# Latent attention: where the products of branch a stand among the steps of the heads

## The chip, the cores and the metric

The kernel runs on one core of one Trainium2 chip. The metric is the device time of one execution in microseconds (us). The kernel before was timed three times: 971.97, 972.13 and 969.66 us, median 971.97 us. The profiled execution, a fourth one, took 969.88 us, of which its instructions span 968.1 us.

## The reference

One decoder layer on 1024 tokens of width 1024, float32. The part that matters:

```python
o_a = stick_breaking_attention(...)             # branch a, 8 heads
y_a = (o_a * silu(sb_z)) @ w_branch_a           # 512 -> 1024
q, k, v = ...                                   # from the two latents, 8 heads, 64 + 32 wide
sc = (q_nope @ k_nope + q_pe @ k_pe) * scale    # causal
o_b = softmax(sc) @ v                           # branch b, latent attention
y_b = (o_b * silu(mla_z)) @ w_branch_b          # 512 -> 1024
merged = sigmoid(g_a) * y_a + sigmoid(g_b) * y_b
x = x + gate * (merged @ w_out); return rmsnorm(x, final_norm_gain)
```

## The kernel before, in words

Every product of float32 values is made of three products of rounded parts (high x high, high x low, low x high), each 128 rows by up to 512 columns on TensorE (PE). The kernel goes through its stages in this order: the opening, branch a's attention with other projections beside it, the two latents, the up-projections, the eight heads of the latent attention, then one closing stage that makes y_b, merges it with y_a, multiplies by w_out and normalizes.

**The products of branch a.** y_a is made by eight jobs, one for each block of 128 output columns, each of two units of 512 tokens: 16 units in all. A unit is 12 products (4 blocks of 128 inputs, three parts), L301, `ps_g<-oa,whi` and `ps_g<-oa,wlo`. VectorE (DVE) then multiplies the unit's result by the gate read back from DRAM (`gl<-ps_g,gl`, L1019) and the sync engine's DMA queue (SP) stores it (`ya_d<-gl`, L1020). Before a job its weights are loaded (L274), DVE rounds them (L88) and GpSimd (POOL) takes the rest (L96). Two buffers hold gates, two hold loaded weights, two PSUM tiles (`ps_g`) hold results. The units come out of a generator, one at each call of `advance(filler, 1)`; two are called in the up-projection (UQF, L1126), the others among the heads.

**The heads.** `mla_heads` (L1207) is a generator too. Each head `h` has eight rows `i` of 128 queries. A row of scores (L1166) is, for each piece of up to 512 keys, three products (L1179 to L1181) into one of two `ps_s` tiles, from which DVE takes the scaled, masked score and the running maximum (L1182); ScalarE (ACT) takes the exponential (L1191). Four rows later PE turns the row in blocks of 128 (L702, `ps_t<-ident,sc`), ACT and DVE write its two parts out (L86, L96), and after each second row PE multiplies by the values (L719, `ps_o<-wth,vb`). Each head begins with eight turns of its queries (L1156). The sums of the exponentials are turned (L1200), go to DRAM and come back spread over the rows (`rs_d`, `rb`, L1203 and L1204); in the last head this is done by halves, POOL multiplies by the gate (L1237) and DVE scales the output (L1238).

The generator stops 128 times, at each row of scores and at each row that is turned. The loop at the end counts these steps. FP is a list of steps at which one more unit is called; from step IA on a unit is called inside `issue_after(anchor)`, which puts each of the unit's instructions on PE behind the last product of the heads issued so far. Below IA, and on all other engines, a scheduler that runs when the program is built may move the unit to an earlier place. What is left of the units after the heads is called at once (L1294).

**The closing stage.** y_b has eight jobs of two units each as well (L301, `<-ob,whi`), whose tiles lie in memory that the heads gave back. For each unit SP loads a gate (`gbl`, L1309) and the stored y_a (`yal`, L1310), DVE multiplies and adds (L1311, L1312), ACT and DVE split the sum. Between these loads SP also issues the loads of w_branch_b (`raw`, L274) and of w_out (`rawo`, L1326), all in one order fixed when the program is built.

Of the kernel before, what the change touches and what calls it, by code (L numbers as in the profile page):

```python
# [48 lines left out]
def hybrid_layer(ctx: ExitStack, tc: tile.TileContext, x, c, positions, w_ada, b_ada, norm_gain, w_in,  # L49
# [853 lines left out]
    with tc.tile_pool(name="latw", bufs=2, **RW, side="right") as lp:  # L903
# [32 lines left out]
        for t in range(NT):  # L936
# [13 lines left out]
            v = small.tile([P, 2], F32, name="vl", tag="vl")  # L950
# [325 lines left out]
            pump()  # L1276

    step, done, total = 0, 0, 2 * len(yajobs) - len(UQF) - UQE
    FP = [int(v) for v in "1 1 5 7 33 36 43 91 103 123 124 132 132".split()]
    IA = 110  # L1280
    heads = mla_heads()
    while True:
        if not advance(heads, 1):
            break
        step += 1
        want = sum(step >= v for v in FP) if FP else min(total, total * step // YSTEPS)
        if want > done:
            if step >= IA:
                with tc.issue_after(anchor[0].ins):
# [137 lines left out]
```

## Time and profile before

| | |
|---|---|
| runs of the kernel before | 971.97, 972.13, 969.66 us |
| profiled execution: time, span | 969.88 us, 968.1 us |
| PE busy, weight loads (PEld) busy | 98%, 85% of the span |
| DVE, ACT, POOL busy | 65%, 45%, 30% |
| chain that ended last | PE 93%, DMA 4%, DVE 1% |
| heads of the latent attention | from about 667 to 831 us |
| closing stage | from about 831 us to the end |

Times in the rows are us from the start of the span. PE's products overlap: a row of 0.39 us may be followed by the next after 0.23 us, so PE looks busy even where it could go faster; the spacing of starts says more than the busy time. A row "[0.88 <-ACT whi L86]" means that the engine sat idle that long before it and what ended the wait. PEclk is the granted clock of PE, 1.00 for 2.4 GHz and 0.50 for 1.2 GHz. DMA is the mean busy share of the 16 DMA engines.

### The profile page before, as it was taken

What the parts mean: (1) busy time and instruction counts of PE and PEld (TensorE: products, weight loads), DVE (VectorE), ACT (ScalarE), POOL (GpSimd) and SP (SyncE); (2) the same over time, 40 slices, a digit from 0 to 9 for tenths busy, and PEclk for the clock granted to TensorE, in tenths of its full rate; (3) what the DMA queues carried; (4) which work ended last, traced back from release to release, by engine and by line L of the source; (5) the groups of instructions that cost most, each with busy time, mean ns of one, the idle gap of its engine ahead of it and who ended that gap; (6) DMA issues with size and microseconds to landing.
All of it is one profiled execution on the core that took longest, in us unless ns stands there. A gap on an engine that the chain in (4) does not pass through costs nothing.

```text
span 968.1 us, 14331 instructions
## 1 busy us (share of the span) xinstructions
PE 945.7 (98%) x5132; PEld 818.4 (85%) x5132; DVE 633.2 (65%) x1277; ACT 440.2 (45%) x991; POOL 287.8 (30%) x271
## 2 busy tenths in 40 slices
PE   4999999999999999999999999999999999989997
PEld 4888888888888888888888999988899998868886
DVE  5757747586747873584564544964699997696654
ACT  5454433353435343444352423643588885342211
POOL 1010145444634554445352001611121441001222
PEclk9999999999999999999999999999999999999999
DMA  9911643215321322113123301689553422792233
GB/s 307 338 74 44 221 149 99 77 44 163 98 66 44 115 71 77 25 53 98 56 86 111 99 2 33 226 280 291 162 155 102 115 86 88 262 357 96 71 120 99
DMA packets 112711, 122.38 MB, mean 126 GB/s; under 512 B 14928, under 2 KB 81597, under 8 KB 112256
## 3 DMA queue, kind: packets, MB, share of 16 engines
q1 hardware_dynamic: 112550, 121.44, 40.1%
q8 instruction: 41, 0.67, 0.3%
q14 instruction: 30, 0.25, 0.1%
q10 hardware_dynamic: 90, 0.02, 0.0%
HBM read 86.80 MB, written 34.64 MB: 125 GB/s over the span
## 4 chain that ended last, share of the span: by engine, by line
PE 93%; DMA 4%; DVE 1%; ACT 0%; issue 0%; SPq 0%; POOL 0%; DVEq 0%; ACTq 0%; POOLq 0%
PE ps_g L301 37%; PE ps_o L719 7%; PE ps_t L702 7%; PE ps_g L944 3%; PE ps_g L1363 3%; PE ps_s L1363 3%; PE ps_t L1363 3%; PE ps_s L945 3%; PE ps_g L553 3%; PE ps_s L553 2%; PE ps_s L1179 2%; PE ps_s L1181 2%; PE ps_s L1180 2%; PE ps_s L750 2%; PE ps_s L749 2%; PE ps_t L1059 2%
## 5 line engine op out<-in xcount | busy, mean ns | idle before, releaser
L301 PE MATMUL ps_g<-hh,whi 128*128 128x512 f32 x448 | 177.7, 397 | 0.0
L301 PE MATMUL ps_g<-hl,whi 128*128 128x512 f32 x448 | 176.9, 395 | 0.0
L301 PE MATMUL ps_g<-hh,wlo 128*128 128x512 f32 x448 | 175.7, 392 | 0.0
L753 DVE TENSOR_TENSOR_SCAN surv<-surv,diag 128x128 f32<-128x128 f32 (+3 forms) x64 | 109.6, 1717 | 47.6 <-ACT surv L751 46.5
L96 POOL TENSOR_TENSOR wlo<-raw,whi 128x1024 fp32r<-128x1024 f32 (+1 forms) x36 | 78.0, 2166 | 113.9 <-DVE whi L88 36.3
L96 DVE TENSOR_TENSOR wtl<-ps_t,wth 128x512 fp32r<-128x512 f32 (+1 forms) x192 | 101.7, 548 | 11.0 <-ACT wth L86 10.0
L757 POOL TENSOR_TENSOR beta<-beta,surv 128x127 f32<-128x127 f32 (+3 forms) x64 | 83.6, 1307 | 59.4 <-DVE surv L753 58.8
L86 ACT ACTIVATE wth<-ps_t 128x512 fp32r<-128x512 f32 (+1 forms) x192 | 90.2, 491 | 21.0 <-PE ps_t L702 18.2
L301 PEld LDWEIGHTS ps_g<-hh,wlo 128*128 128x128 f32 x448 | 84.2, 188 | 17.0
L301 PEld LDWEIGHTS ps_g<-hh,whi 128*128 128x128 f32 x448 | 84.2, 188 | 16.0
L301 PEld LDWEIGHTS ps_g<-hl,whi 128*128 128x128 f32 x448 | 84.4, 188 | 15.0
L393 ACT ACTIVATE ev<-ps_g 128x512 f32<-128x512 f32 x32 | 19.2, 600 | 103.7 <-PE ps_g L301 103.7
L88 DVE CAST whi<-raw 128x1024 fp32r<-128x1024 f32 (+1 forms) x38 | 24.9, 656 | 54.1 <-PE ps_g L301 43.7
L1191 ACT ACTIVATE sc<-sc,mx 128x128 f32<-128x128 f32 (+3 forms) x64 | 49.3, 771 | 14.9 <-DVE mx L1182 14.8
L1369 POOL TENSOR_TENSOR xr<-xr,fgain 128x512 f32<-128x512 f32 (+1 forms) x17 | 21.0, 1233 | 112.4 <-ACT yr L1368 108.2
L751 ACT ACTIVATE surv<-ps_s 128x512 f32<-128x512 f32 (+2 forms) x96 | 47.2, 493 | 12.1 <-PE ps_s L750 7.4
L752 ACT ACTIVATE beta<-ps_s 128x512 f32<-128x512 f32 (+2 forms) x96 | 47.6, 498 | 4.5 <-POOL beta L757 4.3
L86 ACT ACTIVATE otmp<-ps_o 64x256 f32<-64x256 f32 x64 | 24.3, 379 | 47.8 <-PE ps_o L719 46.9
L702 PE MATMUL ps_t<-ident,sc 128*128 128x128 f32 x288 | 44.8, 274 | 0.1
L756 POOL MEMSET beta<- 128x1 f32 x64 | 6.7, 104 | 128.0 <-ACT beta L752 125.0
L702 PE MATMUL ps_t<-ident,beta 128*128 128x128 f32 x288 | 43.0, 275 | 0.0
L731 POOL TENSOR_TENSOR oga<-oga,zs 64x256 f32<-64x256 f32 x32 | 36.0, 1126 | 20.2 <-DVE oga L729 19.0
(422 smaller groups left out, 2372.3 us busy)
## 6 DMA issues: line engine op xcount, KB each, us to landing
raw<-in_w_in SPq DMA_DIRECT2D x35, 512.0 KB, 4.0
wa<-in_w_ada SPq DMA_DIRECT2D x12, 512.0 KB, 6.5
x<-in_x SPq DMA_DIRECT2D x8, 512.0 KB, 6.0
v_d<-vo SPq DMA_DIRECT2D x8, 512.0 KB, 4.7
v<-v_d SPq DMA_DIRECT2D x4, 1024.0 KB
ga_d<-ev SPq DMA_DIRECT2D x16, 256.0 KB, 3.0
wg<-in_w_ada SPq DMA_DIRECT2D x8, 512.0 KB, 3.6
gb_d<-ev SPq DMA_DIRECT2D x16, 256.0 KB, 2.0
```

What stands on the lines that cost most here:

```text
L86: nc.scalar.activation(o, i, AF.Copy)
L96: (nc.vector if eng == "v" else nc.gpsimd).tensor_tensor(out=o, in0=full, in1=rd(hi), op=ALU.subtract)
L301: nc.tensor.matmul(out=ps, lhsT=w[:, k, :], rhs=m[k][:, hsl(hf)], start=n == 0, stop=n == last)
L553: nc.tensor.matmul(out=accu[q][unit], lhsT=m[:, tsl], rhs=w[:, 0:512], **fl)
L702: anchor[0] = nc.tensor.transpose(out=pt[:, b * P:(b + 1) * P], in_=w[:, (j0 + b) * P:(j0 + b + 1) * P], identity=ident)
L719: anchor[0] = nc.tensor.matmul(out=po[:, qs], lhsT=vtile(j), rhs=wts[j // 4][n][:, j % 4, qs], start=j == 0 and n == 0, stop=j == i and n ...
L751: nc.scalar.activation(surv[:, c0:c0 + wc], ps[:, 0:wc], AF.Sigmoid, scale=-0.125)
L752: nc.scalar.activation(beta[:, c0:c0 + wc], ps[:, 0:wc], AF.Sigmoid, scale=0.125)
L753: scan[0] = nc.vector.tensor_tensor_scan(out=surv[:, 0:w][:, ::-1], data0=surv[:, 0:w][:, ::-1], data1=diag1[:, S - w:S][:, ::-1], initial ...
L757: nc.gpsimd.tensor_tensor(out=beta[:, 0:w - 1], in0=beta[:, 0:w - 1], in1=surv[:, 1:w], op=ALU.mult)
L1191: nc.scalar.activation(sc[:, 0:w], sc[:, 0:w], AF.Exp, bias=mx[:, len(chunks) - 1:len(chunks)] if CH else mx[:, 0:1], scale=-1.0, accum_ou ...
L1363: nc.tensor.matmul(out=ps[:, 0:wc], lhsT=m[k][:, tsl], rhs=w[:, k, cs], start=k == 0 and i == 0, stop=k == KD - 1 and i == 2)
```

## The change

Two numbers of the loop change: the list of steps FP and the step IA. Sixteen units remain, and every instruction of them.

```diff
     step, done, total = 0, 0, 2 * len(yajobs) - len(UQF) - UQE
-    FP = [int(v) for v in "1 1 5 7 33 36 43 91 103 123 124 132 132".split()]
-    IA = 110
+    FP = [int(v) for v in "1 5 20 34 44 53 62 71 80 89 103 123 132".split()]
+    IA = 30
     heads = mla_heads()
     while True:
         if not advance(heads, 1):
             break
         step += 1
         want = sum(step >= v for v in FP) if FP else min(total, total * step // YSTEPS)
         if want > done:
             if step >= IA:
                 with tc.issue_after(anchor[0].ins):
                     advance(filler, want - done)
             else:
                 advance(filler, want - done)
         done = want
```

In PE's order before, six of the 16 units stand ahead of the heads' first product, five among the rows of the first head, and the last five behind the last product of the scores of head 7. In the order after, five stand ahead, eight are spread from the third head to the seventh, and three stand behind the last scores.

The first place is on PE, where the heads begin. Before, the end of the sixth unit (`ps_g<-oa`), the turns of the queries (L1156), the first two rows of scores (`ps_s<-kt`), and the seventh unit:

```order
L301 MATMUL ps_g<-oa_5771,wlo 128x512
L1156 MATMUL ps_t<-ident,qn 96x128 x12
L1179 MATMUL ps_s<-kt_5753,qh 128x128
L1180 MATMUL ps_s<-kt_5753,qh 128x128
L1179 MATMUL ps_s<-kt_5753,qh 128x256
L1180 MATMUL ps_s<-kt_5753,qh 128x256
L1181 MATMUL ps_s<-kt_5753,ql 128x128
L1181 MATMUL ps_s<-kt_5753,ql 128x256
L1156 MATMUL ps_t<-ident,qn 96x128 x4
L301 MATMUL ps_g<-oa_5768,whi 128x512
L301 MATMUL ps_g<-oa_5772,whi 128x512
```

And after, behind the fifth unit:

```order
L301 MATMUL ps_g<-oa_5771,wlo 128x512
L1156 MATMUL ps_t<-ident,qn 96x128 x8
L1179 MATMUL ps_s<-kt_5753,qh 128x128
L1180 MATMUL ps_s<-kt_5753,qh 128x128
L1179 MATMUL ps_s<-kt_5753,qh 128x256
L1180 MATMUL ps_s<-kt_5753,qh 128x256
L1181 MATMUL ps_s<-kt_5753,ql 128x128
L1181 MATMUL ps_s<-kt_5753,ql 128x256
L1179 MATMUL ps_s<-kt_5753,qh 128x384
L1180 MATMUL ps_s<-kt_5753,qh 128x384
L1181 MATMUL ps_s<-kt_5753,ql 128x384
L1179 MATMUL ps_s<-kt_5753,qh 128x512
```

The rows of scores now follow each other with no unit of branch a between them, and none comes until 29 pieces of scores are through.

The second place is on PE too, at the end of the heads, around the turn of the second half of the last head's sums (L1200). Before, the last unit of branch a (`<-oa`) stands around it; the eight products L719 that follow begin with the last row shown:

```order
L702 MATMUL ps_t<-ident,sc 128x128 x4
L301 MATMUL ps_g<-oa_5772,whi 128x512
L301 MATMUL ps_g<-oa_5768,wlo 128x512
L301 MATMUL ps_g<-oa_5769,whi 128x512
L1200 MATMUL ps_t<-ident,rs 4x128
L301 MATMUL ps_g<-oa_5773,whi 128x512
L301 MATMUL ps_g<-oa_5769,wlo 128x512
L301 MATMUL ps_g<-oa_5770,whi 128x512
L301 MATMUL ps_g<-oa_5774,whi 128x512
L301 MATMUL ps_g<-oa_5770,wlo 128x512
L301 MATMUL ps_g<-oa_5771,whi 128x512
L719 MATMUL ps_o<-wth,vb 128x256
```

And after, a whole unit of branch b (`<-ob`, its first product ahead of the rows shown) stands ahead of it:

```order
L301 MATMUL ps_g<-ob_6355,whi 128x512
L301 MATMUL ps_g<-ob_6351,wlo 128x512
L301 MATMUL ps_g<-ob_6352,whi 128x512
L301 MATMUL ps_g<-ob_6356,whi 128x512
L301 MATMUL ps_g<-ob_6352,wlo 128x512
L301 MATMUL ps_g<-ob_6353,whi 128x512
L301 MATMUL ps_g<-ob_6357,whi 128x512
L301 MATMUL ps_g<-ob_6353,wlo 128x512
L301 MATMUL ps_g<-ob_6354,whi 128x512
L301 MATMUL ps_g<-ob_6358,whi 128x512
L301 MATMUL ps_g<-ob_6354,wlo 128x512
L1200 MATMUL ps_t<-ident,rs 4x128
```

Before, eight products of branch a (six shown and two more behind the eight L719) and all of branch b come behind L1200; after, all of branch a and twelve products of branch b come ahead of it. Sixteen products L719 stand behind it in both.

The third place is on SP in the closing stage, the loads up to the one of the seventh job's weights (`raw<-in_w_branch_b`). Before:

```order
L1344 DMA fgain<-in_final_norm_gain 128x1024
L1310 DMA yal<-ya_d_5780 128x512
L1309 DMA gbl<-gb_d_88 128x512
L1310 DMA yal<-ya_d_5781 128x512
L1309 DMA gbl<-gb_d_88 128x512
L274 DMA raw<-in_w_branch_b 128x4x128
L1326 DMA rawo<-in_w_out 128x512
```

And after:

```order
L1344 DMA fgain<-in_final_norm_gain 128x1024
L1310 DMA yal<-ya_d_5781 128x512
L1309 DMA gbl<-gb_d_88 128x512
L1310 DMA yal<-ya_d_5781 128x512
L274 DMA raw<-in_w_branch_b 128x4x128
L1326 DMA rawo<-in_w_out 128x512
L1309 DMA gbl<-gb_d_89 128x512
```

The load of the second half of the sixth y_a block now stands ahead of the weights; counted from the first `yal`, the weights' load is the 35th transfer in place of the 34th.

## Rows read from the trace of the kernel before

**Rows 1.** Busy time by stretch: PE, PEld, DVE, ACT, POOL, then PEclk, DMA share, GB/s.
```profile
700.00:800.00 100.00, 99.88 (x736) 91.64 (x737) 91.62 (x264) 87.26 (x214) 29.96 (x12) 1.00 0.41 112
...
831.00:838.00 7.00, 7.00 (x32) 5.79 (x32) 3.83 (x7) 2.40 (x5) 0.00 (x0) 1.00 0.74 219
838.00:869.00 31.00, 28.51 (x123) 22.32 (x122) 28.90 (x48) 13.86 (x24) 0.00 (x0) 1.00 1.03 360
```
**Rows 2.** The chain that ended last, in the heads: start, length, what, how many.
```profile
659.95 7.71 PE ps_g L301 x34
...
750.21 0.44 PE ps_t L1156 x4
...
751.45 1.07 PE ps_o L719 x9
...
766.61 0.44 PE ps_t L1156 x4
```
**Rows 3.** The same chain, one product of 512 columns of the scores.
```profile
782.50 0.23 PE ps_s L1180
```
**Rows 4.** PE's instructions where the heads' stage ends: start, length, line, operation.
```profile
822.82 0.27 PE L1200 MATMUL ps_t<-ident,rs 128*4 128x128 f32 x1
```
**Rows 5.** The chain that ended last, at the end of the heads.
```profile
823.13 0.28 ACT rst L86
823.42 1.41 DMA rs_d<-rst
824.84 2.89 DMA rb<-rs_d
827.87 1.30 POOL rb L1237
...
830.52 0.35 DVE ogb L1238
830.89 0.32 SPq L1310
```
**Rows 6.** POOL's last addition of the heads.
```profile
829.24 0.98 POOL L727 TENSOR_TENSOR ogb<-ogb,otmp 64x256 f32<-64x256 f32 x1
```
**Rows 7.** SP's issues in the closing stage, around the seventh job's weights.
```profile
855.71 0.38 SPq L274 DMA_DIRECT2D raw<-in_w_branch_b  x1
856.39 0.33 SPq L1326 DMA_DIRECT2D rawo<-in_w_out  x1
```
**Rows 8.** PE where the closing stage waits; in brackets the idle time before.
```profile
849.61 0.73 PE L301 MATMUL ps_t<-ob,whi 128*128 128x512 f32 x2 [0.88 <-ACT whi L86]
...
862.69 1.19 PE L301 MATMUL ps_g<-ob,whi 128*128 128x512 f32 x4 [1.53 <-ACT whi L86]
```
**Rows 9.** PE where the heads begin.
```profile
667.49 1.47 PE L1156 MATMUL ps_t<-ident,qn 128*96 128x128 f32 x12
668.77 0.33 PE L1179 MATMUL ps_s<-kt,qh 96*128 96x128 f32 x1
...
669.50 0.50 PE L1181 MATMUL ps_s<-kt,ql 96*128 96x128 f32 x2
```
**Rows 10.** DVE in the first head.
```profile
676.12 0.68 DVE L1182 CUSTOM_DVE_ANT_0 sc<-ps_s,cmask 128x512 f32<-128x512 f32 x1
...
685.60 0.69 DVE L1019 TENSOR_TENSOR gl<-ps_g,gl 128x512 f32<-128x512 f32 x1 [1.47 <-DMA gl<-ga_d]
```
**Rows 11.** SP: the load of the keys of head 7; PE: the first product of head 7.
```profile
773.59 0.45 SPq L1097 DMA_DIRECT2D kt<-k_d  x1
...
790.52 0.30 PE L1179 MATMUL ps_s<-kt,qh 96*128 96x128 f32 x1
```
**Rows 12.** By stretch as Rows 1: a fallen clock; the waits of Rows 8.
```profile
41.40:44.80 3.40, 3.40 (x11) 2.72 (x10) 1.90 (x6) 2.23 (x5) 0.00 (x0) 0.50 1.08 361
...
844.00:850.00 6.00, 5.12 (x23) 3.91 (x22) 5.26 (x10) 2.86 (x5) 0.00 (x0) 1.00 1.00 327
858.00:864.00 6.00, 4.47 (x19) 3.19 (x19) 5.87 (x11) 2.56 (x5) 0.00 (x0) 1.00 1.08 360
```

## The prediction

> **What bounds the kernel now.** I read the page first, then busy time by stretch, then the chain that ended last, then the timelines of SP, PE, POOL and DVE around two places that the chain named.
>
> The heads of the latent attention are bound by PE, but less tightly than its busy time says. From 700 to 800 us PE is busy 99.88 of 100 us [rows 1], yet one head lasts 16.40 us from turn of queries to turn of queries (750.21 to 766.61) [rows 2], and its products need less. At the spacing of starts in the chain's pieces a turn takes 0.44/4 = 0.11 us, a product by values 1.07/9 = 0.119 us [rows 2], a product of scores of 512 columns 0.23 us [rows 3]. A head has 8 + 36 + 1 turns (5.0 us), 32 products by values of 256 columns and 8 of 128 (about 4.5 us) and scores worth 27 products of 512 columns (6.2 us): 15.7 us. So PE stands still or is slowed for about 0.6 us in each head. DVE, busy 91.62 of the 100 us [rows 1], is the engine that it waits for.
>
> The closing stage is bound otherwise. From 838 to 869 us the DMA engines are full (share 1.03), DVE is busy 28.90 of 31 us, and PE only 28.51 [rows 1]. PE waits twice for weights that a DMA brings, at 849.61 (0.88 us) and at 862.69 (1.53 us) [rows 8]; behind the second wait it runs without one to the end. The stream of transfers begins at 830.89 with the first `yal` load (the SPq piece at the end of the group) [rows 5]: it waits for DVE's last scaling of the heads' output, because its tile lies in memory that the heads still use. That scaling hangs on the turn L1200 at 822.82 [rows 4]: 823.13 copy, 823.42 to DRAM, 824.84 back, 827.87 POOL's product [rows 5], 829.24 POOL's addition [rows 6], 830.52 DVE [rows 5]. So the first `yal` comes 830.89 - 822.82 = 8.07 us after L1200, the seventh job's products 862.69 - 830.89 = 31.80 us after the first `yal`, and the rest follows. What is late here is L1200, not PE's amount of work.
>
> **The change part by part.** No instruction is added or removed, only places differ. A unit is 12 products of 7.71/34 = 0.227 us [rows 2], 2.72 us.
>
> (1) The end of the heads. L1200 has six plus two products of branch a fewer behind it and twelve of branch b more ahead of it: 20 products, 20 x 0.227 = 4.54 us of PE's work now stand ahead of L1200 that stood behind it. All of PE's work up to L1200 has to be done first, so L1200 comes 4.54 us later, and with it the first `yal`, the stream and the end. What PE did ahead of time does not shorten the stage, for its two waits grow by as much. Bounds: 0, if the stream does not decide (a rival below), and 4.54. I take 4.54, since the wait of 1.53 us shows that it decides already [rows 8].
>
> (2) The stream. One more transfer of 256 KB stands ahead of the seventh job's weights. Issues follow each other there at 856.39 - 855.71 = 0.68 us [rows 7]. Bounds 0 and 1.36 us (a second displaced), taken 0.68 us.
>
> (3) The start of the heads. Before, a unit of 2.72 us stands between the second and the third row of scores, and four more follow. Without them PE waits for its helpers: from the first turn to the first score product 668.77 - 667.49 = 1.28 us, to the first low product 669.50 - 667.49 = 2.01 us [rows 9], with only eight turns (0.88 us) to fill it; then each piece of scores waits for one of two `ps_s` tiles, which DVE frees at 0.68 us for 512 columns [rows 10] while PE needs 3 x 0.23 = 0.69. DVE must also write out the queries' and the weights' low parts, so it sets the pace until the rows' backlog is there. I walked the order up to the seventh row: PE needs 8.2 us, DVE lets it through in about 10.3. Bounds: 0.4 us (1.28 - 0.88, the bare first wait) and 5 us (two heads at DVE's pace). Taken 2.1 us plus the 0.4 us: 2.5 us.
>
> (4) The middle. Eight units from step 34 to step 103 lie in 70/16 = 4.4 heads. DVE gets about 0.8 us of extra work per unit (a product of 0.69 us [rows 10], half a rounding) against PE's 2.72, so it falls behind less. Bounds: all of the 0.6 us per head gone (-2.6 us); or, on the other side, DVE stops at a gate that has not landed, 1.47 us in the worst row [rows 10], at each unit with half of it reaching PE (+3 us), since scores' reductions are queued behind it and PE waits for their `ps_s`. Taken -1.7 us (0.6 to 0.2 us per head). POOL's and SP's parts of a unit I cost at nothing: POOL is busy 29.96 of 100 us [rows 1]; SP may stop for a gate's buffer, and loads of keys and values are queued behind, but the keys of head 7 are issued at 773.59 and wanted at 790.52 [rows 11]. Without that cover each late load would cost its delay.
>
> PE's busy share leaves nothing to win in the middle (99.88 of 100), the spacing of starts 0.6 us of each 16.4 [rows 1, 2]. The Trainium skill, "Perfetto Trace Analysis", section "Identifying the Most-Contended Engine", says that busy matmul time is a poor measure and busy time of weight loads a better one. By it PEld's 91.64 of 100 [rows 1] would leave 1.4 us per head, 6.0 us over the 4.4 heads; with that in place of (4) the sum below would be 1.7 us. The rows of starts decide for me; this is the reading that speaks for a gain.
>
> Sum: 4.54 + 0.68 + 2.5 - 1.7 = 6.0 us. The profiled execution took 969.88 us, so 975.9 us; the median of the three runs lies 2.1 us above it at 971.97, and on that scale the forecast is 978.0 us. Ends of the range: 4.54 + 0 + 0.4 - 2.6 = +2.3 (974.3) and 4.54 + 1.36 + 5 + 3 = +13.9; all bad ends together are unlikely, so 984 is its upper end here.
>
> **The rivals.**
>
> A, faster: the heads give back their 0.6 us in every one of the eight heads and the start costs only its 0.4 us, while the end is bound by PE, not by the stream: -4.8 + 0.4 = -4.4 us, 967.6 us. For it: the spread units stand exactly where DVE is the late engine. Against it: three heads get no unit, and PE's waits for weights at 849.61 and 862.69 [rows 8].
>
> B, no change: the stream does not hang on L1200, because transfers catch up when PE comes to it further ahead (before, DMA share is only 0.74 from 831 to 838 [rows 1]). Then (1) and (2) fall away and 2.5 - 1.7 = +0.8 us stays: 972.8 us. For it: that slack of 7 x 0.26 = 1.8 us. Against it: 1.8 us is less than 4.54, and afterwards the share is 1.03.
>
> C, slower still: PE's longer idle time in the closing stage lowers its clock. The first wait would grow from 0.88 to about 0.88 + 4.54 + 0.5 = 5.9 us. Row for the price: a stretch of 3.40 us at a granted clock of 0.50 [rows 12], in which half the products go through, 1.7 us lost. One fall after the fifth job is hidden by the second wait; one after the seventh job's wait reaches the end: 978.0 + 1.7 = 979.7 us. In the waits of before the clock stayed at 1.00 [rows 12]; they were short, so they do not exclude it. With the start at its worst (+2.5) it is 982.2 us. The Trainium skill, "TensorE: Matmul & The Clock Gate", section "Part 1: The HAM clock gate (the "warmup" mystery)", states this rule: the slow level is the default and activity releases it. By that rule the time would be C's.
>
> **How the numbers follow.** Forecast 978.0 us, chance 0.58, its own range 974.3 to 984. C 0.14, B 0.16, A 0.12. A measurement of this kernel tells a difference from none at about 0.3%, 2.9 us. Slower by more: C and nine tenths of the forecast, 0.14 + 0.53 = 0.67; within: B and the rest, 0.21; faster: A, 0.12. The range for 8 in 10 leaves out A and the worst ends: 972 to 983 us.
>
> **What the profile would show.** If right: in the timeline of PE, L1200 of the last half 4 to 6 us later than 822.82; from it to the first `yal` about 8 us as before; PE's two idle times in the closing stage together near 8 us in place of 2.4; after them the same length to the end. In the first head PE's starts with gaps, 2 to 3 us in all; from the third head to the seventh about 0.2 us of loss per head beside the units. It is wrong if the first `yal` is not later, if PE's idle time in the closing stage does not grow, or if the stretch from the first turn of queries to L1200 loses or gains more than 3 us against the products that stand in it. A granted clock under 1.00 between 845 and 875 us would speak for C.

## The result and the profile after

The changed kernel takes 980.55 us (median of 4 runs, 978.14 to 981.89), the kernel before 971.75 beside it: a ratio of 1.0092 (95% interval 1.0077 to 1.0108), 8.8 us slower. The forecast was 978.0 us. The profiled execution of the changed kernel is its slowest one, 981.89 us with a span of 980.0. A second profile of it, taken later (run e12, span 976.3, 978.07 us), has the same opening as the profile of before to within 0.3 us, so it is the better one to compare with; both are used.

The end of the heads in the first profile of the changed kernel, by the timelines of PE, SP, POOL and DVE (start, length, engine, line, operation, in brackets the idle time before):
```profile
834.85 0.27 PE L1200 MATMUL ps_t<-ident,rs 128*4 128x128 f32 x1
...
835.45 0.26 SPq L1203 DMA_DIRECT2D rs_d<-rst  x1
836.62 0.45 SPq L1204 DMA_DIRECT2D rb<-rs_d  x1
...
839.52 1.29 POOL L1237 TENSOR_TENSOR rb<-rb,zsb 128x512 f32<-128x512 f32 x1 [5.77 <-DMA rb<-rs_d]
840.88 0.98 POOL L727 TENSOR_TENSOR ogb<-ogb,otmp 64x256 f32<-64x256 f32 x1
...
841.90 0.43 DVE L1238 TENSOR_TENSOR ogb<-ogb,rb 128x256 f32<-128x256 f32 x1 [0.63 <-POOL ogb L727]
...
842.35 0.32 SPq L1310 DMA_DIRECT2D yal<-ya_d  x1
```
It is the chain of [rows 4 to 6], step for step: L1200 comes 12.03 us later (1.47 of them arose ahead of the units, since line 944 begins at 535.31 and not at 533.84), and the first `yal` 842.35 - 834.85 = 7.50 us behind it (8.07 before).

PE's waits in the closing stage of the same profile, which answer to [rows 8]:
```profile
859.22 0.72 PE L301 MATMUL ps_t<-ob,whi 128*128 128x512 f32 x2 [2.74 <-ACT whi L86]
...
861.26 0.79 PE L301 MATMUL ps_t<-ob,wlo 128*128 128x512 f32 x1 [0.85 <-DVE wlo L96]
...
873.51 1.19 PE L301 MATMUL ps_g<-ob,whi 128*128 128x512 f32 x4 [0.43 <-ACT whi L86]
...
875.66 0.50 PE L301 MATMUL ps_g<-ob,wlo 128*128 128x512 f32 x1 [0.96 <-DVE wlo L96]
```
They sum to 4.98 us, against 2.41 before. Busy time by stretch (columns as in [rows 1]; the last but two is the granted clock), first one row of the kernel before, then the changed one:
```profile
650.00:700.00 50.00, 50.00 (x271) 42.48 (x269) 28.64 (x76) 21.64 (x51) 5.15 (x4) 1.00 0.78 240
```
```profile
669.99:673.41 3.42, 3.42 (x13) 2.94 (x14) 1.99 (x7) 1.77 (x7) 0.00 (x0) 0.50 1.00 271
673.41:700.00 26.59, 26.17 (x183) 23.00 (x182) 23.60 (x69) 22.29 (x55) 0.00 (x0) 1.00 0.39 108
700.00:800.00 100.00, 99.55 (x667) 88.89 (x666) 79.12 (x217) 67.84 (x167) 27.45 (x13) 1.00 0.47 136
838.00:869.00 31.00, 27.36 (x112) 21.52 (x111) 24.23 (x42) 13.58 (x24) 2.27 (x2) 0.94 0.86 302
861.14:864.55 3.41, 3.29 (x8) 2.61 (x9) 3.41 (x7) 1.39 (x3) 0.00 (x0) 0.50 1.05 387
```
The granted clock fell to 0.50 twice where it had been 1.00 before (the row from 650 to 700, and [rows 12]): at 669.99, in the first rows of the heads, and at 861.14, behind the long waits of the closing stage. In the heads DVE and ACT have become much less busy (79.12 and 67.84 of 100 us), because products of units now fill part of the 100 us; PE's busy time is that of [rows 1] but for 0.33 us.

**Where the time went.** Each profile is cut at four of PE's instructions: the first product of line 944 (the stage ahead of the heads), the first turn of queries, the second L1200, the last L1200. Of before, beside [rows 4, 9], from PE's timeline:
```profile
533.84 0.34 PE L944 MATMUL ps_g<-wch,hh 128*128 128x384 f32 x1
...
712.42 0.28 PE L1200 MATMUL ps_t<-ident,rs 128*8 128x128 f32 x1
```
The same four of the changed kernel in its second profile:
```profile
533.62 0.34 PE L944 MATMUL ps_g<-wch,hh 128*128 128x384 f32 x1
...
664.83 1.08 PE L1156 MATMUL ps_t<-ident,qn 128*96 128x128 f32 x8 [0.18 <-DMA qn<-q_d]
...
698.04 0.28 PE L1200 MATMUL ps_t<-ident,rs 128*8 128x128 f32 x1
...
831.15 0.27 PE L1200 MATMUL ps_t<-ident,rs 128*4 128x128 f32 x1
```
What lies ahead of line 944 is left out: the change does not touch it, and line 944 begins anywhere from 533.05 to 537.78 in the profiles. From each of the first three lengths the products of the units that stand in it are taken off at the prediction's 0.227 us; the last one stays as it is, and "moved" is what it has lost in units. Example, the rest of the heads: 831.15 - 698.04 = 133.11 us with 144 such products, before 822.82 - 712.42 = 110.40 with 52; 133.11 - 110.40 - 92 x 0.227 = +1.83. So for every run (us against the profile of before; "moved" is the work of units that stands ahead of the last L1200 and did not before; the tail is the units behind the last scores, "unhooked" the edit of e4):

| Kernel | moved | opening | first rows | rest of heads | last L1200 to end | sum | medians |
|---|---|---|---|---|---|---|---|
| changed, first profile | +4.54 | +0.7 | +3.5 | +1.8 | -0.1 | +10.4 | +8.8 |
| changed, again (e12) | +4.54 | +0.3 | +1.9 | +1.8 | -0.1 | +8.4 | +8.6 |
| e1 tail alone | +4.54 | -0.1 | 0.0 | 0.0 | +1.4 | +5.9 | +5.7 |
| e2 start and middle | 0 | +0.7 | +1.9 | +2.1 | -0.9 | +3.8 | +4.5 |
| e3 two units back | +4.54 | 0.0 | +1.9 | +1.1 | +0.6 | +8.0 | +9.2 |
| e4 changed, unhooked | +4.54 | +0.2 | +1.9 | +1.8 | -2.0 | +6.5 | +4.9 |
| e5 changed, b behind | +1.82 | +0.6 | +1.9 | +1.8 | -1.6 | +4.5 | +5.0 |
| e6 ten, none, six | -2.72 | +0.1 | +0.9 | 0.0 | +3.5 | +1.9 | +1.6 |
| e7 before, unhooked | 0 | 0.0 | 0.0 | 0.0 | -1.4 | -1.4 | -0.7 |
| e8 ten, none, six, unhooked | -2.72 | 0.0 | +0.9 | 0.0 | +3.1 | +1.3 | +0.9 |
| e9 before, less DVE | +0.45 | 0.0 | 0.0 | +1.6 | -2.0 | 0.0 | +1.3 |
| e10 changed, less DVE | +4.99 | +0.4 | +1.9 | +2.0 | +1.6 | +10.8 | +11.5 |
| e11 before, unhooked, POOL | 0 | 0.0 | -0.1 | 0.0 | -0.4 | -0.5 | +1.4 |

The two columns of the heads repeat to 0.1 us wherever the order in that stretch is the same and the clock stayed at 1.00 (first rows: before, e1 and e7; e2, e4, e5 and e12). The last stage differs by more than a microsecond from execution to execution: before and e2 have the same tail and differ there by 0.9. Its single entries say little under 1.5 us; the medians of many runs decide there.

### The profile page after: what moved, and what is told of

It reads as the page before. It is cut to its first block, busy times and chain, and to the rows that moved or that the text cites. A ratio compares the mean times of both kernels' runs of the same rounds, so it can differ in the third digit from the quotient of the medians.

```text
span 980.0 us, 14323 instructions
## 1 busy us (share of the span) xinstructions
PE 953.4 (97%) x5132; PEld 822.9 (84%) x5132; DVE 633.1 (65%) x1277; ACT 440.4 (45%) x991; POOL 288.3 (29%) x271
## 4 chain that ended last, share of the span: by engine, by line
PE 93%; DMA 3%; DVE 2%; issue 1%; ACT 0%; POOL 0%; SPq 0%; DVEq 0%; POOLq 0%
PE ps_g L301 36%; PE ps_o L719 7%; PE ps_t L702 6%; PE ps_g L944 3%; PE ps_g L1363 3%; PE ps_s L1363 3%; PE ps_t L1363 3%; PE ps_s L945 3%; PE ps_g L553 2%; PE ps_s L553 2%; PE ps_t L301 2%; PE ps_s L1179 2%; PE ps_s L750 2%; PE ps_s L1181 2%; PE ps_s L749 2%; PE ps_s L1180 2%
## 5 line engine op out<-in xcount | busy, mean ns | idle before, releaser
L1182 DVE CUSTOM_DVE_ANT_0 sc<-ps_s,cmask 128x512 f32<-128x512 f32 (+2 forms) x64 | 37.3, 584 | 9.8 <-PE ps_s L1181 6.4
```

## The experiments

Each was timed beside the kernel before on one chip. e1 to e3 and e6 change the list of steps, and which of them are tied:
```diff
-    FP = ... "1 1 5 7 33 36 43 91 103 123 124 132 132"    IA = 110
+e1  FP = ... "1 1 5 7 33 36 43 44 45 62 80 123 132"       tied: 62 80 123
+e2  FP = ... "1 5 20 34 48 62 76 89 103 123 124 132 132"  tied: 34 to 124
+e3  FP = ... "1 1 5 7 33 36 53 71 80 89 103 123 132"      tied: 53 to 123
+e6  FP = ... "1 1 5 7 33 36 43 44 123 124 132 132 132"    tied: from 123
-            if step >= IA:
+            if step in TIED:
```

**e1.**

> Eleven units early as in the kernel before, the tail as in the changed kernel (three units behind step 110), only two units (steps 62 and 80) in the middle: the end of the heads by itself. Theory (the last row of maxima, L1200, sets when the stream of the closing stage begins): 20 products more ahead of the last L1200, +4.5 us, one transfer +0.7, two units in the middle at most -0.8: 975.5 to 977.5 us, and from the last L1200 to the first yal about 8 us, PE's idle time in the closing stage up from 2.4 to 6 us or more. Rival B (the stream catches up, all of the loss is at the start of the heads): within 1.5 us of before, 970.5 to 973.

977.82 us against 972.13, ratio 1.0057 (1.0041 to 1.0073): +5.7 us, as the theory has it. PE and SP, timelines:
```profile
830.27 0.27 PE L1200 MATMUL ps_t<-ident,rs 128*4 128x128 f32 x1
...
837.77 0.32 SPq L1310 DMA_DIRECT2D yal<-ya_d  x1
```
Counted from line 944 (536.88 in e1), L1200 comes 4.4 us later, the first `yal` again 7.50 us behind it, and no other column of the heads changes by more than 0.1. PE's waits in the closing stage sum to 5.99 us. So the tail alone is worth about two thirds of the loss, and the two units in the middle of the heads give nothing back.

**e2.**

> The first heads as in the changed kernel (no unit in the first rows), six units in the middle, the tail of the kernel before (five units): start and middle without the end. Theory: the start costs 5 to 6 us (stalls and a fall of the clock at about 670 us, as in the changed kernel), six units in the middle give back 2 to 3: 974 to 976 us. Rival (the end costs nothing, all of the 8.8 us come from the start): 979 to 981 us. Rival (the end is all of it): 970 to 972 us.

976.63 us, 1.0052 (1.0038 to 1.0066): +4.5, 0.6 above the theory's band and far from both rivals. The start costs 0.7 + 1.9 = 2.6 us, where 5 to 6 were expected; the fall of the clock, which the 5 to 6 held and which did not come here, is 1.6 us of that by the table. The middle costs 2.1 us, where a gain was expected.

**e3.**

> Two of the units put back among the first rows of scores, five in the middle, the tail as in the changed kernel. Theory: with work for PE in the first rows the clock stays at 1.00 there and the stalls of 664 to 680 us halve, the end still costs 5.2: 975.5 to 978 us. Rival (the start's loss is the clock's alone, and two units keep it up): the start loses nothing, 975 us or less. Rival (the start's loss is DVE's pace and only moves to the next rows): 979 to 981 us.

981.33 us, 1.0094 (1.0078 to 1.0110): the last rival. Two units put back at the start bring nothing, the first rows lose 1.9 us with them as without. The clock stayed at 1.00 there.

**e4.** The tiles of the first half of `wo` are made before the load tiles, which so come to lie where the scores were:
```diff
     wos = []
+    pre = [fin.tile([P, KD, 512], F32R, name=f"wo{n}0") for n in "hl"]
...
-            hi, lo = [fin.tile([P, KD, 512], F32R, name=f"wo{n}{hf}") for n in "hl"]
+            hi, lo = [fin.tile([P, KD, 512], F32R, name=f"wo{n}{hf}") for n in "hl"] if hf else pre
```

> The changed kernel, with the two tiles of the first half of wo made ahead of the closing stage's load tiles, so that these lie where the scores were and not where the heads' output is scaled: the stream need not wait for DVE's last scaling behind L1200. Theory (the stream's begin at the first yal decides): the first yal some 5 us or more earlier against the last product by values, PE's four idle times in the closing stage (5 us) mostly gone: 974 to 977 us. Rival (the stream is as fast as the DMA engines and DVE let it, or PE bounds the closing stage): within 1.5 us of the changed kernel's 980.5.

977.04 us, 1.0060 (1.0047 to 1.0073): 3.5 us less than the changed kernel, at the edge of the theory's band (974 to 977). PE and SP, timelines:
```profile
831.74 0.27 PE L1200 MATMUL ps_t<-ident,rs 128*4 128x128 f32 x1
...
834.69 0.38 SPq L1310 DMA_DIRECT2D yal<-ya_d  x1
...
856.13 0.50 PE L301 MATMUL ps_t<-ob,wlo 128*128 128x512 f32 x1 [1.85 <-DVE wlo L96]
...
868.43 1.20 PE L301 MATMUL ps_g<-ob,whi 128*128 128x512 f32 x4 [0.43 <-ACT whi L86]
...
870.59 0.50 PE L301 MATMUL ps_g<-ob,wlo 128*128 128x512 f32 x1 [0.96 <-DVE wlo L96]
```
The first `yal` follows L1200 by 2.95 us in place of 7.50, so it did wait for memory. But 4.55 us of earlier stream save only 1.74 us of waiting (3.24 against 4.98): behind it stands DVE, which writes the low parts.

**e5.** The changed kernel, with each call of branch b's products tied behind the last value product:
```diff
     for n in range(16):
-        advance(filler, 1)
+        with tc.issue_after(anchor[0].ins):
+            advance(filler, 1)
```

> The changed kernel, but the first twelve products of branch b held behind the last product by values, so that L1200 has them no longer ahead of it. Theory (the place of the last L1200 sets the stream and the end): L1200 and the first yal 2.7 us earlier against the last turn of scores, the end 2 to 3 us earlier than the changed kernel: 977 to 979 us. Rival (PE is the bound there, the same products only change places): within 1 us of 980.5.

976.89 us, 1.0055 (1.0033 to 1.0076): 3.7 us less, the theory's side, slightly more than it asked. PE's timeline:
```profile
832.04 0.27 PE L1200 MATMUL ps_t<-ident,rs 128*4 128x128 f32 x1
...
857.91 0.74 PE L301 MATMUL ps_t<-ob,whi 128*128 128x512 f32 x2 [1.14 <-ACT whi L86]
...
870.33 1.21 PE L301 MATMUL ps_g<-ob,whi 128*128 128x512 f32 x4 [1.20 <-ACT whi L86]
```
No work was taken away: 2.72 us of it went behind L1200, and PE waits 2.34 us there in place of 4.98. The clock stayed at 1.00.

**e6.**

> The kernel before with one unit of branch a taken from the first heads and put behind L1200: ten early, none in the middle, six at the end. Theory (L1200 decides; the two waits for weights in the closing stage, 2.4 us, can be filled; one unit less at the start costs about 0.5 us): L1200 2.2 us earlier, 969.5 to 971 us. Rival (the start's loss per unit taken is as large as what the end gives): 971.5 to 973 us.

973.50 us, 1.0018 (1.0004 to 1.0032): slower, past the rival's band. L1200 did come earlier, by 1.7 us (2.72 less 1.0 at the start). The stream did not. PE's L1200 and SP's issues behind it:
```profile
824.58 0.27 PE L1200 MATMUL ps_t<-ident,rs 128*4 128x128 f32 x1
...
828.44 5.79 SPq L1020 DMA_DIRECT2D ya_d<-gl  x2
834.84 0.38 SPq L274 DMA_DIRECT2D raw<-in_w_branch_b  x1
...
835.88 0.37 SPq L1310 DMA_DIRECT2D yal<-ya_d  x1
```
The stores of branch a's last two units (one of each) now stand in SP's queue ahead of `raw` and `yal`, and the first `yal` comes 11.30 us behind L1200. Putting work behind L1200 helps only until its own stores hold the stream.

**e7 and e8.** The edit of e4 on the kernel before, and that together with e6.

> The kernel before, with the two tiles of the first half of wo made ahead of the closing stage's load tiles, as in the run of the changed kernel with that edit. Theory (the first yal waits for DVE's last scaling only through its memory): the first yal 3 to 4.5 us earlier, PE's waits of 0.88 and 1.53 us gone: 969.3 to 970.5 us. Rival (weights and their low parts come no earlier, DVE and the DMA engines set their pace): 971.5 to 972.5 us.

> Both edits on the kernel before: ten, none and six units, and the tiles of wo ahead of the load tiles. Theory: the waits of the closing stage go once only, so it is no faster than the better one of the two alone, 969.3 to 971 us. Rival (each gives its own part, the stage still waits after one): 967.5 to 969 us.

e7: 971.21 against 971.90, 0.9990 (0.9974 to 1.0005), not told apart from no change and between the two expectations; the first `yal` comes 5.54 us behind L1200 in place of 8.07, and one wait is left, again DVE's:
```profile
826.68 0.27 PE L1200 MATMUL ps_t<-ident,rs 128*4 128x128 f32 x1
...
832.22 0.38 SPq L1310 DMA_DIRECT2D yal<-ya_d  x1
...
865.99 0.50 PE L301 MATMUL ps_g<-ob,wlo 128*128 128x512 f32 x1 [1.26 <-DVE wlo L96]
```
e8: 972.78, 1.0017 (1.0001 to 1.0032), slower than e7 alone and outside both expectations; its first `yal` is held by the stores as in e6 (two `ya_d` from 825.45, `yal` at 832.98, 11.39 us behind L1200), and memory no longer matters.

**e9.** `AVP = 7` set to 2, on the kernel before: from the third head on ACT and POOL add the halves of the values' products in place of DVE.

> The kernel before, with the addition of the two halves of a value product taken from DVE in the heads from the third on (ACT copies, POOL adds, as it already does for the last head): 0.41 us off DVE four times per head, 1.6 of its some 15 us. Theory now (PE does not wait in the middle heads, its 0.6 us per head are the spacing of the scores' first products behind turns): heads still 16.4 us each, within 1.5 us of before. Rival, step (4) of the prediction (PE waits there for DVE): up to 0.6 us off each of the five middle heads, 968.5 to 970 us.

972.17 us against 970.87, 1.0013 (1.0001 to 1.0025). Busy time by stretch, before and then e9:
```profile
700.00:795.00 95.00, 94.88 (x696) 86.90 (x697) 87.06 (x251) 82.94 (x204) 29.31 (x12) 1.00 0.42 115
```
```profile
700.00:795.00 95.00, 94.63 (x692) 86.40 (x691) 80.37 (x232) 85.71 (x217) 39.27 (x28) 1.00 0.43 115
```
DVE has 6.69 us less to do, and the heads are 1.6 us longer in sum, not shorter. That speaks against DVE as what PE waits for in the middle heads; alone it doesn't show it, since ACT (2.77 us more) and POOL (9.96 us more) took the work over.

**e10.** `AVP = 0`, on the changed kernel.

> The changed kernel with the same edit for all heads, from the first on. Theory (the first two heads without units run at the pace of DVE): the stall of the first rows, 4.4 us up to the second L1200 without the clock's fall, shrinks by 1 to 2 us: 978 to 979.5 us. Rival (the first rows wait for the chain from scores over the exponentials to the turns, by ACT and by latency, not for DVE's amount of work): no change or slower, 980 to 982 us, since ACT has more to do.

982.39 us, 1.0121 (1.0104 to 1.0137): the rival, at the upper end of its band. The first rows lose 1.9 us as they did. The test is weak for the very first rows, since the first of these additions stands at 679.10 in the changed kernel.

**e11.** e7, and branch b's low parts written by POOL (`le="v"` to `le="p"`).

> The kernel before with the tiles of wo ahead of the load tiles (as e7) and the low parts of branch b's weights written by POOL in place of DVE. Theory (once the stream starts earlier, the one wait left in the closing stage, 1.4 us before the seventh job's low products, is for DVE's queue): that wait gone, 968.5 to 970 us. Rival (POOL's rounding takes longer than DVE's, so the low parts come no earlier): 971 to 974 us.

972.25 us, 1.0023 (1.0013 to 1.0034), the rival's side. The wait for low parts shrank to 0.56 us, although POOL takes 1.68 us to write them where DVE took 0.68. But 2.02 us of waiting for the high parts stands ahead of the same job: ACT begins to write them 860.04 - 821.97 = 38.07 us behind L1200, in e7 862.83 - 826.68 = 36.15. So the weights came no earlier than in e7. No version faster than the kernel before came out.

**e12.**

> The changed kernel once more, unaltered, for a second look at its clock. Theory (the fall of the clock at 670 us in the first profile happened by chance in that execution; it stood in none of the four other profiles that begin the heads without units; the fall at 861 us comes with the long waits of the closing stage and stood in each profile with that tail): no fall between 660 and 680 us, one between 850 and 870, the stall up to the second L1200 4.4 us, not 6.4; 978 to 981 us. Rival (the changed kernel's own order makes it fall at 670 each time): a fall there again, 980.5 to 982.5 us.

980.50 us against 971.88. Its clock at the two places, by stretch:
```profile
660.00:680.00 20.00, 19.10 (x115) 15.75 (x114) 13.93 (x40) 11.15 (x28) 1.28 (x1) 1.00 0.72 212
...
857.24:860.65 3.41, 2.98 (x7) 2.41 (x8) 3.41 (x7) 1.57 (x3) 0.00 (x0) 0.50 1.05 386
```
As the theory has it: no fall at the start of the heads, one in the closing stage. The 4.4 us that it names for the loss up to the second L1200 are not what the table's count gives, 0.3 + 1.9 = 2.2 us.

## Why the prediction came out as it did

Direction and most of the size were right, 6.0 us forecast against 8.8. One step had the wrong sign, and it makes up more than the difference; that the forecast is off by no more than that owes something to luck, since (2) and (3) were 1.0 us too large together.

(1) The end of the heads: right. e1 moves the tail alone and L1200 comes 4.4 us later (4.54 forecast), the end 5.7; e5 takes twelve of the twenty products back and wins 3.7. What PE did ahead of L1200 did not shorten the stage behind it: with 20 products fewer there (4.54 us) it lasts as long as before (-0.1 us). The reason given was only half right. The waits did not grow to near 8 us but to 4.98; the rest went into a clock at 0.50 from 861.14 to 864.55, half of 3.41 us, 1.7.

(2) One more transfer in the stream, 0.68 us: not to be seen. The seventh job's weights are issued 865.51 - 842.35 = 23.16 us behind the first `yal`, before 855.71 - 830.89 = 24.82 [rows 5, 7], and in e2, with the tail of before, 23.1. What executions differ by is larger than the term.

(3) The start, 2.5 us: the size was right, 0.3 + 1.9 = 2.2 us in e12. That DVE's pace is the reason was shown for a part at most. The view of PE's waits in e12 from 664 to 832 us has, for the start of the heads,
```profile
PE ps_s L1179 <- DVE mx L1182: 0.6, 3, 0.3
PE ps_s L1179 <- ACT qh L86: 0.2, 1, 0.2
PE ps_t L1156 <- DMA qn<-q_d: 0.2, 1, 0.2
```
so of the 1.9 us of the first rows 0.6 are put down to DVE and 0.2 to ACT (the third line is ahead of the first turn); the rest has no releaser in the view. e10 took work from DVE, and the loss stayed. One unit fewer costs 0.9 us (e6), three or five fewer 1.9 (e3, e12), so it does not grow with each. In the first profile 2.0 us came on top: 0.4 us ahead of the first turn of queries, which waited 0.63 us for its load in place of 0.18, and 1.6 us in the first rows, with the fall of the clock at 669.99 (half of its 3.42 us is 1.7). That fall stands in one of the six profiles that begin the heads so (changed twice, e2, e4, e5, e10).

(4) The middle, -1.7 us: this step failed. It measured +1.8. From the first turn of queries to the last L1200, e12 loses 1.9 + 1.8 = 3.7 us against its products: more than the 3 us that the prediction had named as a sign of being wrong. The 0.6 us per head had been found by taking PE's products at their spacing from a head's length, and were then put down to DVE because DVE was the busiest helper. The view of PE's waits would have answered it. For the kernel before, from 668 to 822 us, it holds no row, only its heading:
```profile
core 0 of [0], span 968.1 us
engine line waited for: us in total, times, longest us
```
No wait that the profile ascribes to an engine was there to be filled: e1 put two units into these heads and got 0.0 us back, and e9 unburdened DVE and got less than nothing. About half of the 0.6 us was not idle time but a wrong price. The prediction counted scores by their columns, so that a product of 128 columns would cost 0.23/4 = 0.058 us. From PE's timeline of the kernel before, in the head that it took for its sum:
```profile
757.92 0.28 PE L1180 MATMUL ps_s<-kt,qh 96*128 96x128 f32 x1
758.03 0.28 PE L1181 MATMUL ps_s<-kt,ql 96*128 96x128 f32 x1
758.14 0.33 PE L1179 MATMUL ps_s<-kt,qh 96*128 96x256 f32 x1
```
They start 0.11 us apart, and a head has six of them: 0.3 us. (The prediction's own terms, 5.0 + 4.5 + 6.2, leave 0.7 of the 16.40 us, not 0.6.) What the rest consists of was not found. Another sum of that step does not come out either: 1.47 us at each of eight units, half of it reaching PE, is 5.9 us and not 3, so its bad end was set too low.

Why the heads lose 1.8 us was not found: the same view of e12 names 0.4 us of it between the second and the last L1200. 1.4 us stand between the second and the fifth L1200, among which six of the eight units lie. The loss is 0.0 with two units in e1, 1.1 with five in e3, 2.1 with six in e2 and 1.8 with eight, so it comes with the spreading, but not at a fixed price for each. That units' products cost more than 0.227 us among the heads is no sufficient reason: it would take 0.247 us in e12, and e1, with 20 more of them there, loses nothing.

The reading that stood against the forecast, that PE's time in loading weights shows room (91.64 of 100 us), fell with the same runs. By the measure that the Trainium skill, "Perfetto Trace Analysis", section "Identifying the Most-Contended Engine", prefers, the prediction's estimate was 6.0 us there; the heads gave none.

The rivals. A, the heads giving back everywhere, fell with (4). B, a stream that does not hang on L1200, fell with e1 and e5. C was half right: the clock did fall in the closing stage, in all six profiles with the tail of three units and branch b's products ahead of L1200 (changed twice, e1, e3, e4, e10) and in none of the eight others. The rule weighed there (the Trainium skill, "TensorE: Matmul & The Clock Gate", section "Part 1: The HAM clock gate (the "warmup" mystery)") agrees with these rows. C added its 1.7 us to a sum in which the waits took all of the work done ahead; they took 2.6 of 4.5, and the fall took most of the rest. So C's 979.7 us lies nearer to the 980.55 than the forecast does, but by a sum with the same wrong (4) in it. The prediction called a fall behind the fifth job hidden; e5, without one, ends 1.5 us sooner behind its L1200 than the changed kernel although it has twelve more products there, which speaks against that, though e5 changes both at once and 1.5 us is what single entries of that column may differ by.

The sum of e12: 4.54 + 0.3 + 1.9 + 1.8 - 0.1 = 8.4 us, against the forecast's 4.54 + 0.68 + 2.5 - 1.7 = 6.0. Shown by runs are the price of the end (e1, e5) and that start and middle each cost about 2 us; the reasons of the latter two stay open.

## What to carry to other kernels

Before filler is moved, find the last instruction on which the next stage's transfers hang: each product put ahead of it costs its full time there, and idle time or a lower clock behind it eats what was done ahead. Time that is left when an engine's instructions are taken from a stage's length is not a wait; price it as a gain only if the view of waits names a releaser for it, and take the price of short products from rows of their own. And filler can be moved too far the other way as well: its own stores, in the same queue, then hold the loads of the next stage (11.30 us in place of 8.07).

## What the runs showed of the hardware that was not expected

The clock fell to 0.50 (1.2 GHz) late in a kernel whose clock was at 1.00 (2.4 GHz) before the change, from 650 to 700 us as in the waits of the closing stage. In the closing stage it fell at or right behind waits of 1.85 us (e4), 2.74 and 0.85 (changed) and 4.60 (e1), each time for 3.41 us; in e10 it fell during a wait of 4.46 us, for 6.83 us. In the kernel before, with waits of 0.88 and 1.53 us, it stayed, and so it did in e11 with a wait of 2.02 us, longer than the one behind which it fell in e4: the length of the longest wait alone does not decide. At the start of the heads the same order kept it at 1.00 in five profiles and let it fall in one, at a cost of 1.6 us.
